# One inference step of a hybrid encoder on one core: two-tile stores, a weight sum in another block, and two pools for the down-projection

## The chip, the core and the metric

The kernel runs on one core of a Trainium2 chip. A core has a matrix engine (TensorE, PE in the profile, with its weight loads as PEld), a vector engine (VectorE, DVE), a scalar engine (ScalarE, ACT), a general one (GpSimd, POOL), and SyncE (SP), which issues most DMA transfers here. Each engine works through its own instructions in order and waits for the others by semaphores. The metric is the device time of one launch in microseconds (us); of several runs the median is given. The 0.2% below which two medians of this kernel can't be told apart is about 4.6 us.

## The reference

One layer over a prompt of 2048 tokens and 8 short sequences of 16 tokens, which together fill one more tile: 17 tiles of 128 tokens with 1024 features, all in float32.

```python
qm, km, vm, om, ip, fp, qa, ka, va = split_in(x @ w_in)
hm, C1, n1, m1 = mlstm_chunkwise(qm, km * 128**-0.5, vm, ip + b_i, log_sigmoid(fp + b_f), C0, n0, m0, chunk)
hm = sigmoid(om) * head_norm(hm, g_mlstm_norm)           # 4 heads x 128
ha = sliding_window_attention(rope(qa), rope(ka), va, sinks)   # 8 query heads, 2 key heads x 64
mix = concat(hm, ha) @ w_out
h = layer_norm(alpha * x + mix)
u = h @ w_up                                              # 1024 -> 5632 = value | gate
c = b_conv + sum(ext(u)[:, j:j + T] * w_conv[j] for j in range(3))
y = layer_norm(alpha * h + (silu(gate(c)) * value(c)) @ w_down)   # 2816 -> 1024
```

The outputs are y, the new mLSTM states, the new keys and values, and the last rows of u.

## The kernel before, in words

The work has four stages, which follow one another on TensorE.

1. *Input projection*, 0 to about 621 us. Four blocks of four token tiles (`IBLOCKS`; the tile of the short sequences, number 16, belongs to the first). Within a block, five groups g = 0 to 4: two for queries and keys of the mLSTM, one for the attention's queries (zqa), one for the output gates (zog), one for the mLSTM's values (zv). Each group is a 2x2 block product done with seven products instead of eight (Strassen's scheme in Winograd's form), in the order s = 1, 7, 6, 2, 5, 3, 4, into three PSUM banks (`i_product`, the matmuls of L713). `i_after` combines the products, and `i_store` (L757 and following) writes each finished quarter, 2 token tiles by 256 columns, to DRAM. `i_direct` (L739) computes the narrow columns: the gates' inputs and the attention's keys and values (`i_keys`, whose store is L750).
2. *Output projection*, about 622 to 899 us (L223 to L225), with the first layer norm.
3. *Up-projection* with the convolution, about 899 to 1827 us (L1883); its result, value times gate, goes to DRAM (`zf`, store L1971).
4. *Down-projection*, about 1827 to 2300 us (L2091; L2099 copies a product that two results share into a second PSUM bank, and L2122 adds into the results' accumulators `yacc`), again with seven products.

Each float32 operand is split into a high and a low part (L218 casts the high part on ScalarE, L219 subtracts it on VectorE), and three matmuls are done for each product.

Into the first stage the tiles' own work is woven as generators that a planner (`Chains`) advances between steps of two matmul groups, by costs and due times: for each tile an mLSTM chain (gates' logarithms L1007 to L1010, their transposes on TensorE at L1019, the head norm's statistics L1171 to L1178, transposes at L1188, the numerator L1223, the state L1235) and an attention chain (scores, L1332, L1354 and L1355, L1360); for the short sequences `t_sample` (softmax with sinks L1515 to L1527).

The order of TensorE's instructions is written out by hand (a manual schedule). The other engines' instructions are ordered when the program is built, by a list scheduler that takes the program's order, dependences and buffer lifetimes into account; each engine then runs its list in order. SP's list is the queue of nearly all loads and stores: where an issue waits for a buffer or for data, everything behind it waits as well.

Two further parts belong to the change. Down-projection products with the combined quarters of `wdn` need sums of its rows. Four slices of them are formed in the first stage by `d_sums(k, step)`, called after product s = 6 (step 0: two loads of 512 KB into buffers `txy`, L854 and L855), after s = 5 (step 1: four VectorE subtractions, L860 to L863) and after s = 3 (step 2: two stores to `zt`, L865 and L866). The buffers are those of `xr1` and `xr3`, two tiles that the loads of the next block's inputs use too. The pairs (b, g) at which this happens stand in one line of `i_dense`, with nb = 4 blocks:

```python
if (b, g) in ((nb - 2, 1), (nb - 1, 0), (nb - 1, 1), (nb - 1, 2)):
```

And the down-projection reads `zf` back in quarters r1 to r4 (`d_load`, issued at L2013). r1 lies in a buffer of the outer pool `fsb`; r2, r3, r4 and the accumulators `yacc` lie in the pool `dsb`, which is opened when the up-projection's pools `f2sb` and `f3sb` are closed and takes their place in SBUF. The weights of the down-projection come at L2031.

Of the kernel before, what the change touches and what calls it, by code (L numbers as in the profile page):

```python
# [8 lines left out]
F32 = mybir.dt.float32  # L9
# [5 lines left out]
P = 128  # L15
D = 1024
# [5 lines left out]
NT = NPT + 1  # L22
# [18 lines left out]
IBLOCKS = [[0, 1, 2, 3, 16], [4, 5, 6, 7], [8, 9, 10, 11], [12, 13, 14, 15]]  # L41
# [6 lines left out]
HT = 2 * P  # L48
# [157 lines left out]
class Prog:  # L206
# [20 lines left out]
    def run(self):  # L227
        PS = bass.MemoryType.PSUM
        nb = len(OBLOCKS)
        with ExitStack() as es:  # L230
            def enter(*a, **k):
                cm = self.pool(*a, **k)
                return cm.__enter__(), cm
            close = lambda cm: cm.__exit__(None, None, None)
            self.cp = es.enter_context(self.pool("const"))
            self.dp = es.enter_context(self.pool("dram", space=bass.MemoryType.DRAM))
            es.enter_context(self.tc.manual_schedule(engines={mybir.EngineType.PE}))
            self.setup()
            self.wp = es.enter_context(self.pool("wsb"))
            self.dps = es.enter_context(self.pool("dps", 3, PS))  # L240
            self.tp, tcm = enter("tsb", side="right")
            self.tps, tpcm = enter("tps", 5, PS)
            self.xp, xcm = enter("xsb")
            self.mp, mcm = enter("isb")
            chains = Chains(self)
            self.xs, self.gates, self.i_done = {}, {}, 0
            self.i_begin()
            self.warm_up()
            chains.weave(self.i_dense())
            close(mcm)  # L250
            wx, wxcm = enter("wx1sb")
            self.unit_more(wx)
            self.mp, mcm = enter("osb")
            self.o_setup()
            for b in range(nb - 1):
                chains.weave(self.late_done(self.o_block(b)))
            chains.until(NPT - 1)
            chains.drain()
            close(tpcm)
            close(tcm)  # L260
            self.fp, fcm = enter("fsb", side="right")
            self.fup, fpcm = enter("fup", 3, PS)
            self.f_setup()
            dense = self.o_block(nb - 1)
            first = self.f_hT(0)
            next(first)
            n = 0
            for i, _ in enumerate(dense):
                if i >= 2:
                    next(first, None)  # L270

                if i in (4, 7, 10):
                    self.f_tokens(0, *{4: (1,), 7: ("t1",), 10: ("t3", 7, "t2", 6)}[i])

                if i >= 22 and n < (2, 4, 5)[min((i - 22) // 4, 2)]:
                    self.f_next()
                    n += 1
            for _ in first:
                pass
            assert not self.norms  # L280
            close(mcm)
            close(wxcm)
            close(xcm)

            self.wx, wxcm = enter("wx2sb")
            self.f2, f2cm = enter("f2sb")
            self.f3, f3cm = enter("f3sb")
            self.f_ups(n)
            close(f3cm)
            close(f2cm)  # L290
            self.f2, f2cm = enter("dsb")
            self.f_downs()
            for cm in (f2cm, wxcm, fpcm, fcm):
                close(cm)


    def setup(self):
        nc, a, cp, dp = self.nc, self.a, self.cp, self.dp
        self.ident = cp.tile([P, P], F32, name="ident")
        self.eps = cp.tile([P, 1], F32, name="eps")  # L300
        nc.vector.memset(self.eps, EPS)
        self.mhalf = cp.tile([P, 8], F32, name="mhalf")
        nc.vector.memset(self.mhalf, -0.5)
        self.zqk = [dp.tile([8, P, P * len(b)], F32, name=f"zqk{i}") for i, b in enumerate(IBLOCKS)]
        self.zws = [[dp.tile([1 if g < KEPT else 2, P, 4, HT], F32, name=f"zws{g}_{i}") for i in range(4)] for g in range(NG)]
        self.zv = [dp.tile([P, 512], F32, name=f"zv{t}") for t in range(NT)]
        self.zog = [dp.tile([P, 512], F32, name=f"zog{t}") for t in range(NT)]
        self.zqa = [dp.tile([P, 512], F32, name=f"zqa{t}") for t in range(NT)]
        self.zkv = [dp.tile([P, 256], F32, name=f"zkv{t}") for t in range(NT)]
        self.zmix = [dp.tile([KD, P, P * len(b)], F32, name=f"zmix{i}") for i, b in enumerate(OBLOCKS)]  # L310
        self.zh = [dp.tile([P, D], F32, name=f"zh{t}") for t in range(NT)]
        self.zw = [dp.tile([4, P, 1024], F32, name=f"zw{j}") for j in range(NFF)]
        self.zc = [dp.tile([P, 2, len(FBLOCKS[0]) * P], F32, name=f"zc{j}") for j in range(NFF)]
        self.zM = [dp.tile([1, MH, P + 1], F32, name=f"zM{i}") for i in range(2)]
        self.zt = dp.tile([2, NK2, P, D], F32, name="zt")
        self.zf = [dp.tile([NFF, P, len(b) * P], F32, name=f"zf{i}") for i, b in enumerate(FBLOCKS)]
# [274 lines left out]
    def i_dense(self):  # L591
        nc, a = self.nc, self.a
        nb = len(IBLOCKS)
# [34 lines left out]
        for item in self.items:  # L628
# [9 lines left out]
            if item[0] == "t":  # L638
                _, b, ti, e = item
# [22 lines left out]
            _, b, g, s = item  # L662
# [25 lines left out]
            with self.tc.issue_after(behind) if behind and b == 0 else nullcontext():  # L688
                self.advance()

            if (b, g) in ((nb - 2, 1), (nb - 1, 0), (nb - 1, 1), (nb - 1, 2)):

                steps = (6, 5, 3)
                if s in steps:
                    self.d_sums(sums, steps.index(s))
                    sums += s == steps[2]
# [55 lines left out]
    def i_store(self, b, g, i, j, ev):  # L752

        nc = self.nc
        v = ev.rearrange("p (c m) -> p c m", c=2)
        if g < 2:
            f = 4 * i + 2 * g  # L757
            nc.sync.dma_start(self.zqk[b][f:f + 2, :, j * HT:(j + 1) * HT].rearrange("f p m -> p f m"), v)
        else:
            z = (self.zqa, self.zog, self.zv)[g - 2]  # L760
            for c in range(2):
                nc.sync.dma_start(z[IBLOCKS[b][2 * j + c]][:, i * HT:(i + 1) * HT], v[:, c])

    def i_out(self, b, g, i, j, src):

# [1236 lines left out]
    def d_load(self, b, q, u):  # L2002

        h, one = self.d_shape(b)
        if u == 0:
            pool, tag = (self.fp, "hraw") if q == 1 else (self.f2, f"r{q}")
            self.dr[b, q] = pool.tile([P, NK2, 384], F32, name=f"r{q}", tag=tag, bufs=1)
        r = self.dr[b, q]
        k0 = 0 if q in (1, 3) else NK2
        c0 = 0 if q in (1, 2) else h  # L2010
        ks = slice(DUNITS[u][0], DUNITS[u][-1] + 1)
        z = self.zf[b][k0:k0 + NK2][ks].rearrange("k p m -> p k m")
        self.nc.sync.dma_start(r[:, ks, :h], z[:, :, c0:c0 + h])  # L2013
        if one and q in (1, 2):
            self.nc.sync.dma_start(r[:, ks, h:h + one], z[:, :, 2 * h:])
# [46 lines left out]
            self.d_load(*l)  # L2062

    def f_downs(self):
        nc, a, f2 = self.nc, self.a, self.f2
        V, S = nc.vector, nc.scalar
        mm = nc.tensor.matmul
        ln2 = []
# [9 lines left out]
        nb, nu = len(FBLOCKS), len(DUNITS)  # L2078
        ys, ops = {}, {}
# [63 lines left out]
        for g, (b, s, u) in enumerate(self.dseq):  # L2143
# [3 lines left out]
            ts = [*tiles[:np_], *tiles[2 * np_:]] if s == 1 else tiles[np_:2 * np_] if s == 2 else []  # L2147
            if 0 <= u - 2 < len(ts):
                t = ts[u - 2]
                ys[t] = f2.tile([P, D], F32, name="yacc", tag="yacc", bufs=6)  # L2150
                nc.sync.dma_start(ys[t], self.zh[t])
            if g == 3 * nu:
                for n in ("ln2_g", "ln2_b"):
                    t = self.fp.tile([P, D], F32, name="f_" + n, tag="hst", bufs=2)
# [53 lines left out]
```

## Time and profile before

| | |
|---|---|
| median of 3 runs | 2300.78 us (2300.11 to 2303.31) |
| profiled execution, its own time | 2301.44 us |
| its span in the profile | 2299.7 us |
| mean granted TensorE clock | 0.998 |
| busy: PE / PEld / DVE / ACT / POOL | 99% / 91% / 79% / 55% / 12% |
| DMA: moved, mean rate | 631.30 MB, 275 GB/s |

Share of busy time says what an engine did, and not what it waited for. Where one engine is busy nearly all the time, the rows to read are its waits: each gives the engine and line that waited, the engine, tile and line that released it, the time in total, how often, and the longest. The timeline gives an instruction's start in us from the span's start, its length, engine, line, operation, the tiles written and read with their shapes, and in brackets the idle time ahead of it with its releaser; SPq is SP's queue of DMA issues. A window gives the busy time of each engine in a stretch, with the number of instructions, then the granted clock as a share of full speed, the DMA engines' share and the rate in GB/s. DMA rows give the tile written and read, the queue, the number of issues, the size and the median time to landing.

### The profile page before, as it was taken

How to read it: one execution, taken by the hardware profiler on the slowest of the kernel's cores; microseconds unless marked ns; L12 is line 12 of the kernel's file. 1: busy time of each engine (PE TensorE's matmuls, PEld its weight loads, DVE VectorE, ACT ScalarE, POOL GpSimd, SP SyncE). 2: the span in 40 equal slices, each digit the busy share in tenths (PEclk: the TensorE clock that was granted, in tenths of full speed). 3: DMA queues.
4: the chain of work that ended last, by engine and by line, in shares of the span. 5: the costliest groups of instructions: out<-in, count | busy, mean ns of one | idle time of the engine just before them, and what ended most of it. 6: DMA issues, size and time to landing. Idle time of an engine off the chain costs nothing.

```text
span 2299.7 us, 39828 instructions
## 1 busy us (share of the span) xinstructions
PE 2275.3 (99%) x14293; PEld 2090.5 (91%) x14293; DVE 1810.8 (79%) x3068; ACT 1272.3 (55%) x2373; POOL 277.5 (12%) x509
## 2 busy tenths in 40 slices
PE   8999999999999999999999999999999999999998
PEld 8999999989878778999999999999999978888876
DVE  8787677777688888998778777678766786895987
ACT  5453476766776656555656555556555544444442
POOL 0001001010121210211112000003211200200100
PEclk9999999999999999999999999999999999999999
DMA  7988998899998867898777999988998786757742
GB/s 283 318 304 289 302 327 276 276 309 305 324 324 266 279 212 279 300 331 300 280 273 269 305 300 310 311 267 288 320 295 262 248 298 212 251 173 222 256 153 86
DMA packets 302901, 631.30 MB, mean 275 GB/s; under 512 B 48172, under 2 KB 141424, under 8 KB 302704
## 3 DMA queue, kind: packets, MB, share of 16 engines
q1 hardware_dynamic: 298032, 615.06, 79.1%
q0 software_dynamic: 3520, 10.56, 1.5%
q10 hardware_dynamic: 1152, 3.15, 0.4%
q8 instruction: 113, 1.85, 0.3%
q14 instruction: 84, 0.69, 0.1%
HBM read 457.02 MB, written 171.64 MB: 273 GB/s over the span
## 4 chain that ended last, share of the span: by engine, by line
PE 84%; DVE 2%; DMA 2%; issue 0%; ACT 0%; POOL 0%; SPq 0%; DVEq 0%; POOLq 0%; ACTq 0%
PE dps L1883 20%; PE fup L1883 20%; PE dps L713 9%; PE dps L2091 7%; PE fup L2091 6%; PE fht L2091 6%; PE dps L223 3%; PE dps L225 2%; PE dps L224 2%; PE ppo L1360 1%; PE psc L1315 1%; PE ppt L1354 1%; PE dps L739 1%; PE fht L1707 1%; PE pscore L1140 1%; PE pnum L1223 1%
## 5 line engine op out<-in xcount | busy, mean ns | idle before, releaser
L1883 PE MATMUL fup<-hh,uw 128*128 128x384 f32 (+1 forms) x1848 | 478.2, 328 | 0.0
L1883 PE MATMUL dps<-hh,uw 128*128 128x384 f32 (+1 forms) x1848 | 478.0, 328 | 0.0
L1883 PEld LDWEIGHTS fup<-hh,uw 128*128 128x128 f32 x1848 | 330.3, 188 | 0.0
L1883 PEld LDWEIGHTS dps<-hh,uw 128*128 128x128 f32 x1848 | 330.1, 188 | 0.0
L1883 PE MATMUL fup<-hl,uw 128*128 128x384 f32 (+1 forms) x924 | 302.9, 328 | 0.9 <-DVE hl L219 0.9
L1883 PE MATMUL dps<-hl,uw 128*128 128x384 f32 (+1 forms) x924 | 302.8, 328 | 0.0
L1941 DVE SCALAR_TENSOR_TENSOR cc<-u,cw,cc 128x768 f32<-128x768 f32 (+1 forms) x264 | 258.1, 978 | 38.8 <-ACT cc L1939 30.5
L713 PE MATMUL dps<-w,oh 128*128 128x256 f32 x1344 | 254.7, 285 | 0.0
L218 ACT CAST uw<-wraw 128x1024 fp32r<-128x1024 f32 x126 | 123.2, 978 | 230.1 <-PE dps L2091 122.2
L219 DVE TENSOR_TENSOR w<-wraw,w 128x1024 fp32r<-128x1024 f32 (+2 forms) x163 | 186.3, 1150 | 65.7 <-ACT w L218 63.3
L218 ACT CAST w<-wraw 128x1024 fp32r<-128x1024 f32 (+2 forms) x163 | 160.2, 991 | 114.1 <-PE dps L713 53.6
L713 PEld LDWEIGHTS dps<-w,oh 128*128 128x128 f32 x1344 | 210.8, 188 | 11.0 <-issue 8.1
L219 DVE TENSOR_TENSOR uw<-wraw,uw 128x1024 fp32r<-128x1024 f32 x126 | 142.4, 1131 | 62.1 <-ACT uw L218 61.9
L713 PE MATMUL dps<-w,ol 128*128 128x256 f32 x672 | 188.2, 280 | 0.0
L1883 PEld LDWEIGHTS fup<-hl,uw 128*128 128x128 f32 x924 | 173.6, 188 | 1.7 <-DVE hl L219 1.6
L2091 PE MATMUL fup<-uw,fu 128*128 128x512 f32 x726 | 173.9, 396 | 1.3 <-ACT fht L2099 1.3
L1883 PEld LDWEIGHTS dps<-hl,uw 128*128 128x128 f32 x924 | 173.8, 188 | 0.0
L713 PE MATMUL dps<-oh,w 128*128 128x256 f32 x896 | 167.6, 283 | 2.9 <-DVE w L219 2.2
L2091 PEld LDWEIGHTS fup<-uw,fu 128*128 128x128 f32 x726 | 136.5, 188 | 34.3 <-ACT fht L2099 1.8
L2091 PE MATMUL dps<-uw,fu 128*128 128x512 f32 x660 | 164.9, 396 | 0.0
L2091 PEld LDWEIGHTS dps<-uw,fu 128*128 128x128 f32 x660 | 124.2, 188 | 29.7
L713 PEld LDWEIGHTS dps<-oh,w 128*128 128x128 f32 x896 | 140.0, 188 | 9.6 <-issue 4.9
(320 smaller groups left out, 4569.0 us busy)
## 6 DMA issues: line engine op xcount, KB each, us to landing
uw<-zw SPq DMA_DIRECT2D x176, 512.0 KB, 4.8
zw<-uw SPq DMA_DIRECT2D x88, 512.0 KB, 3.5
w<-zws SPq DMA_DIRECT2D x72, 512.0 KB, 6.0
wv<-wup SPq DMA_DIRECT2D x66, 512.0 KB, 5.0
wraw<-wi SPq DMA_DIRECT2D x65, 512.0 KB, 5.2
wraw<-zt SPq DMA_DIRECT2D x60, 512.0 KB, 3.8
wraw<-wdn SPq DMA_DIRECT2D x45, 512.0 KB, 4.5
wraw<-wo SPq DMA_DIRECT2D x40, 512.0 KB, 4.7
```

The costliest lines, as they stand in the source:

```text
L218: nc.scalar.copy(hi, src)
L219: return nc.vector.tensor_sub(lo, src, hi.bitcast(F32)).ins
L223: mm(out, ah, bh, start=start, stop=False)
L224: mm(out, ah, bl, start=False, stop=False)
L225: mm(out, al, bh, start=False, stop=stop)
L713: mm(o, l, r, start=s in (1, 7) and c == k == i == 0, stop=k == 3 and i == 2, skip_group_check=True)
L739: mm(o, x, w, start=k == i == 0, stop=k == KD - 1 and i == 2, skip_group_check=True)
L1140: self.nc.tensor.matmul(ps[:, h], qk[:, 4 + h], qk[:, h], start=True, stop=True)
L1223: nc.tensor.matmul(ps[:, i], sd[:, h], v1[:, h], start=True, stop=t == 0)
L1883: mm(ps, l[:, k], r[:, k], start=s in (1, 7) and k == 0 and i == 0, stop=k == 3 and i == 2, skip_group_check=True)
L1941: V.scalar_tensor_tensor(c[:, v], u[:, i:i + n], w[i], c[:, v], op0=ALU.mult, op1=ALU.add)
L2091: mm(ps, l[:, k, c], r[:, k], start=s in (1, 4, 7) and u == 0 and k == 0 and i == 0, stop=u == nu - 1 and k == n - 1 and i == 2, skip_grou ...
```

## The change

Three parts.

*Stores.* A quarter of groups 2 to 4 covers two neighbouring tiles of a block. Before, each tile has its own DRAM tensor for zqa, zog and zv, and a quarter is stored by two transfers of 128 KB. After, each block has one DRAM tensor with the tile number ahead, and one transfer of 256 KB stores both; readers get slices of it by tile.

*Sums.* The four sums of `wdn` rows stand at (2,1), (3,0), (3,1), (3,2) before and at (1,1), (2,1), (3,0), (3,2) after. The slices are taken in order, so the second sum's slice is now formed at (2,1), and so on.

*Pools.* Instead of one pool `dsb` laid over both pools of the up-projection, `d2sb` (r2 and r3) and `d3sb` (r4 and `yacc`) are opened one after the other in the place of `f2sb` and `f3sb`.

```diff
@@ run
             close(f3cm)
             close(f2cm)
-            self.f2, f2cm = enter("dsb")
+            self.f2, f2cm = enter("d2sb")
+            self.f3, f3cm = enter("d3sb")
             self.f_downs()
-            for cm in (f2cm, wxcm, fpcm, fcm):
+            for cm in (f3cm, f2cm, wxcm, fpcm, fcm):
                 close(cm)
@@ setup
-        self.zv = [dp.tile([P, 512], F32, name=f"zv{t}") for t in range(NT)]
-        self.zog = [dp.tile([P, 512], F32, name=f"zog{t}") for t in range(NT)]
-        self.zqa = [dp.tile([P, 512], F32, name=f"zqa{t}") for t in range(NT)]
+        self.zo = [[dp.tile([len(b), P, 512], F32, name=f"{n}{i}") for i, b in enumerate(IBLOCKS)] for n in ("zqa", "zog", "zv")]
+        self.zqa, self.zog, self.zv = [{t: z[i][ti] for i, b in enumerate(IBLOCKS) for ti, t in enumerate(b)} for z in self.zo]
@@ i_dense
-            if (b, g) in ((nb - 2, 1), (nb - 1, 0), (nb - 1, 1), (nb - 1, 2)):
+            if (b, g) in ((1, 1), (nb - 2, 1), (nb - 1, 0), (nb - 1, 2)):
@@ i_store
-            z = (self.zqa, self.zog, self.zv)[g - 2]
-            for c in range(2):
-                nc.sync.dma_start(z[IBLOCKS[b][2 * j + c]][:, i * HT:(i + 1) * HT], v[:, c])
+            z = self.zo[g - 2][b][2 * j:2 * j + 2, :, i * HT:(i + 1) * HT]
+            nc.sync.dma_start(z.rearrange("c p m -> p c m"), v)
@@ d_load
-            pool, tag = (self.fp, "hraw") if q == 1 else (self.f2, f"r{q}")
+            pool, tag = (self.fp, "hraw") if q == 1 else (self.f3 if q == 4 else self.f2, f"r{q}")
@@ f_downs
-        nc, a, f2 = self.nc, self.a, self.f2
+        nc, a = self.nc, self.a
...
-                ys[t] = f2.tile([P, D], F32, name="yacc", tag="yacc", bufs=6)
+                ys[t] = self.f3.tile([P, D], F32, name="yacc", tag="yacc", bufs=6)
```

## The prediction

> **What bounds the kernel.** I read the page first (busy times, clock), then the waits sorted by length, TensorE's first, then the stretches around each long wait in the timeline and the windows.
>
> ```profile
> PE 2275.3 (99%) x14293; PEld 2090.5 (91%) x14293; DVE 1810.8 (79%) x3068; ACT 1272.3 (55%) x2373; POOL 277.5 (12%) x509
> ...
> PE ppt L1354 <- ACT pth L1355: 2.7, 1, 2.7
> ...
> PE pht L1188 <- ACT hn L1178: 1.3, 3, 0.5
> PE fup L2091 <- ACT fht L2099: 1.3, 1, 1.3
> PE pnum L1223 <- issue: 1.0, 1, 1.0
> ...
> PE ppt L1527 <- POOL scs L1521: 0.8, 1, 0.8
> PE ppt L1354 <- DVE C L1235: 0.8, 1, 0.8
> ```
>
> TensorE (PE) is busy for 99% of the span, and the change leaves its instructions and their order as they are. So time can only come from TensorE's few waits, or go into new ones. The rows are: engine, what waited, who released it, total us, times, longest. The list also has waits for first weights, at the start and in the first block, which the change leaves alone; those shown add up to 7.9 us, and the rest of the text places each.
>
> **The change, part by part.** I compared the order in which the built programs issue on each engine. TensorE's is identical. VectorE (DVE) and ScalarE (ACT) differ only near five places, SyncE's queue (SP) throughout.
>
> *Stores of two tiles by one transfer.* 48 pairs of 128 KB stores become 48 stores of 256 KB. Nearest rows (KB, then median us to landing):
>
> ```profile
> zqk<-zev SPq DMA_DIRECT2D x32, 256.0 KB, 4.1
> ...
> zv<-zev SPq DMA_DIRECT2D x32, 128.0 KB, 4.4
> ```
>
> A transfer of the new size already lands as fast as one of the old. No TensorE wait above comes from these stores or from what reads them, so I take 0 for the 48 issues saved (below: at most a few tenths either way, through the order of SP's queue). They are what lets SP issue other loads earlier; that is counted where those loads are used.
>
> *One weight sum moved from the last block to the second.* A sum is two loads (L854, L855), four VectorE subtractions (L860 to L863) and two stores (L865, L866). Before, the four sums of this stage lie one in the third block, three in the last; after, one in the second, one in the third, two in the last. This touches four places.
>
> Place 1, the last sum of the last block, 498 to 521 us. Windows (PE, PEld, DVE, ACT, POOL busy, then granted PE clock, DMA share, GB/s) and timeline (start, us):
>
> ```profile
> 511.00:514.20 3.20, 0.54 (x6) 0.30 (x4) 1.82 (x3) 1.82 (x6) 1.35 (x1) 1.00 1.04 382
> 514.20:517.40 3.20, 3.20 (x9) 1.26 (x10) 2.05 (x3) 3.20 (x8) 0.38 (x2) 0.51 0.86 297
> ...
> 487.75 0.69 DVE L860 TENSOR_TENSOR txy<-txy 128x512 f32<-128x512 f32 x1 [1.74 <-DMA txy<-wdn]
> ...
> 498.34 0.33 SPq L854 DMA_DIRECT2D txy<-wdn  x1
> ...
> 505.89 0.33 SPq L855 DMA_DIRECT2D txy<-wdn  x1
> ...
> 499.45 0.68 DVE L784 SCALAR_TENSOR_TENSOR zev<-dps,zev 128x512 f32<-128x512 f32 x1
> 503.93 0.69 DVE L860 TENSOR_TENSOR txy<-txy 128x512 f32<-128x512 f32 x1 [3.79 <-DMA txy<-wdn]
> ...
> 512.38 1.28 ACT L1178 ACTIVATE hn<-hn,ms 128x128 f32<-128x128 f32 x4 [2.32 <-POOL ms L1172]
> 513.56 1.04 ACT L1355 COPY pth<-ppt 128x512 f32<-128x512 f32 x2
> 514.18 1.06 PE L1354 MATMUL ppt<-ident,sc 128*128 128x128 f32 x4 [2.66 <-ACT pth L1355]
> ```
>
> VectorE works in order. It stands 3.79 us before L860 for a load that went out only when the previous sum's store had left the buffer, and the norm statistics of the token tile are queued behind. They reach ScalarE late (L1178), which makes L1355 late, for which TensorE waits 2.7 us, after 0.8 us for L1235. Then, in the second window, TensorE works at a granted clock of 0.51: 3.2 us of which 0.49 is lost, 1.6 us. So this place costs 0.8 + 2.7 + 1.6 = 5.1 us. With only two sums in the last block, the later one takes the position that the earlier of the two removed from here had (the row at 487.75: a VectorE wait of 1.74, which delayed no TensorE instruction), and between 499 and 513 VectorE has none of this work. L1178 could then start 3.8 + 0.7 = 4.5 us earlier, at 507.9, and L1355 at 509.1; TensorE wants its result from 514.18 − 2.66 = 511.5 on, so the wait goes altogether. Ends: 0 and −5.1. I take −5.0.
>
> Place 2, the sum of the third block, 306 to 334 us:
>
> ```profile
> 312.37 0.69 DVE L860 TENSOR_TENSOR txy<-txy 128x512 f32<-128x512 f32 x1 [2.76 <-DMA txy<-wdn]
> ...
> 330.51 0.16 DVE L1171 TENSOR_TENSOR mr<-mr,bmv 128x4 f32<-128x4 f32 x1
> ...
> 318.73 1.13 PE L1223 MATMUL pnum<-v,dt 128*128 128x129 f32 x8 [1.00 <-issue]
> ...
> 333.94 0.62 PE L1188 MATMUL pht<-ident,hn 128*128 128x128 f32 x2 [0.48 <-ACT hn L1178]
> ```
>
> Here too VectorE waits for the load, 2.76 us, and TensorE then misses 1.0 us (L1223) and 1.3 us (three waits for L1178): 2.3 us. After, both loads go out some 7 us earlier on SP, and all four subtractions stand earlier in VectorE's order, in front of the running sums of the gates. The wait goes, but a reciprocal that needs ScalarE's exponentials moves ahead of the statistics and costs VectorE about 1 us. So L1171 comes 2.76 − 1.0 = 1.7 us earlier. Ends 0 and −2.3; I take −1.7.
>
> Place 3, the new sum in the second block, 165 to 178 us. In the built order L860 stands right behind L880 at 169.19, the other three between there and L1010, and one more L219 moves ahead of L1010. L1010 ends the gate logarithms that TensorE transposes at L1019, with nothing to overtake it.
>
> ```profile
> DMA to landing us min/median/max: 2.7/5.9/8.2
> ...
> 165.18 0.32 SPq L750 DMA_DIRECT2D zkv<-zev  x1
> ...
> 169.19 0.28 DVE L880 TENSOR_TENSOR zev<-zev,ropet 128x128 f32<-128x128 f32 x1
> ...
> 173.49 1.22 DVE L219 TENSOR_TENSOR w<-wraw,w 128x1024 fp32r<-128x1024 f32 x1
> 174.63 0.38 DVE L1007 SCALAR_TENSOR_TENSOR gl<-gl,gl 128x16 f32<-128x16 f32 x2
> ...
> 175.25 0.17 DVE L1010 SCALAR_TENSOR_TENSOR g<-gl,g 128x16 f32<-128x16 f32 x1
> ...
> 177.95 0.27 PE L1019 MATMUL pgr<-ident,g 128*4 128x128 f32 x1
> ```
>
> The first row is that of this sum's transfers (tile txy). The first load follows the store of 165.18, so goes out at 165.6 and lands 5.9 later, at 171.5; VectorE is there at 169.5: 2.0 us of waiting. Four subtractions at 0.65 (0.69 less overlap) are 2.6, the L219 is 1.14 (to the start of the next): 5.7 us. Against it stand 175.42 to 177.95, 2.5 us of slack, and 0.2 of idle time before an L219. TensorE waits 3.0 us. By the shortest landing (2.7) there is no VectorE wait and it is 1.0; by the longest (8.2) it is 5.3. Below 1.0 is excluded as the instructions stand in front of L1010. I take 3.0, the median's. What queues behind: the weight splits L219, which have three products (8 us) of lead, the sample tile's state update, and on SP the two zt stores, which hold the next weight loads for one or two us. I cost these at nothing; without that cover, see the second rival.
>
> [...]
>
> Place 4, the sample tile's softmax. L551 and the rotary add L881 now stand ahead of L1515.
>
> ```profile
> 246.92 0.15 DVE L1515 SCALAR_TENSOR_TENSOR amx<-amx,nsinkx 128x4 f32<-128x4 f32 x1
> 247.00 1.22 DVE L551 TENSOR_TENSOR wraw<-xr 128x1024 f32<-128x1024 f32 x1
> 248.13 0.68 DVE L881 TENSOR_TENSOR zev<-zev,rb 128x512 f32<-128x512 f32 x1
> ...
> 247.85 0.30 ACT L1516 ACTIVATE aes<-amx,k_sinkx 128x4 f32<-128x4 f32 x1
> ```
>
> L1515 comes 1.1 + 0.6 = 1.7 us later less 0.2 of idle time, at 248.4, but ScalarE began its successor only at 247.85: the chain to L1521, for which TensorE already waits 0.8, is 0.6 us longer. Ends 0 and +1.7; I take +0.6.
>
> *Two pools in the down-projection.* Before, its first new loads sit in a pool laid over both pools of the up-projection, so they wait until the last of those is read, a store:
>
> ```profile
> 1836.60 0.43 SPq L1971 DMA_DIRECT2D zf<-cc  x1
> 1842.33 4.33 SPq L2013 DMA_DIRECT2D r<-zf  x8
> ...
> 1845.78 0.83 ACT L218 CAST fu<-r 128x768 fp32r<-128x768 f32 x1 [4.59 <-DMA r<-zf]
> ...
> 1851.28 1.06 ACT L2099 COPY fht<-fup 128x512 f32<-128x512 f32 x2
> ...
> 1851.91 18.41 PE L2091 MATMUL fup<-uw,fu 128*128 128x512 f32 x78 [1.31 <-ACT fht L2099]
> ...
> 1852.00:1855.20 3.20, 3.20 (x14) 2.62 (x15) 2.20 (x3) 2.98 (x5) 0.00 (x0) 1.00 1.06 409
> ```
>
> ScalarE idles 4.59 us for those loads and then does the casts in one go, so L2099 comes late and TensorE waits 1.31. After, r2 and r3 lie over the first of the old pools alone: in the built order five r loads stand ahead of the last zf store and wait for engines only, some 10 us earlier. ScalarE can cast as the buffers come free, and L2099 is in time. r4 and yacc still wait for the store, and the remaining weights (L2031) now stand behind them on SP; by the 18.41 us of the matmul group that starts at 1851.91 the first of them is needed after 1870, so they are next in line but not late. (The last row is the window behind this wait, with the clock at 1.00.) Ends 0 and −1.3 (the wait shown); I take −1.3.
>
> **Sum.** −5.0 − 1.7 − 1.3 + 0.6 + 3.0 = −4.4 us. The profiled execution took 2301.44 us by its own time (span 2299.7), 0.66 above the median of the runs, 2300.78. So 2297.0 against the profile and 2296.4 against the median. A measurement of this kernel tells 0.2%, 4.6 us, from no change: faster means below 2296.2.
>
> **Rivals.**
> - The new wait at L1019 also halves the clock. For: the wait of 2.7 us at place 1 was followed by 3.2 us at 0.51. Against: after the wait of 1.31 it stood at 1.00 (the window at 1852), and the forecast wait is little longer than 2.7. Price 1.6 us: 2298.0. [...]
> - Slower: the sum is only moved, and SP carries the loss. If the loads land late at place 3 (8.2 us), VectorE loses 4.3 us there, the zt stores hold SP, and weight loads behind them come late as well. Place 1 shows such a blocked queue: 498.34 to 505.89 between two loads of one sum, 5.1 us lost on TensorE. Price: 5.3 at L1019, 1.6 of clock, 5.1 for weights, 1.7 (the upper end) at place 4, against gains of 8.0: +5.7, 2306.5. It decides once the new waits together exceed 8.0. Against: the sum at 487.75 had a VectorE wait of the same kind, and TensorE shows no wait for it in the list.
> - The load lands early, or VectorE catches up: the wait at L1019 stays at 1.0, giving 2294.4. For: SP reaches the load with 48 fewer stores on its way; against: the DMA share of 0.9 to 1.0 in the windows shown.
> - The change doesn't do what it says: the waits are only passed on (place 1's sum waits where it now stands, or r loads come no earlier). Without −5.0 it is 2301.4, without −1.3 it is 2297.7.
>
> **How the numbers follow.** Forecast, 2296.4: 0.40, half of it on either side of 2296.2. Clock halved: 0.18, nearly all of it within 0.2%. Early load: 0.16, faster. Waits passed on: 0.12, within 0.2%. Slower rival: 0.14. Faster 0.20 + 0.16 + 0.04 from the second case with a smaller wait = 0.40; slower (over 2305.4) 0.12, as the slower rival with a little less falls short of that bound; within 0.2% the rest, 0.48. The range from 2292.0 (early load, with place 2 worth 2.3, place 4 nothing, and a little less at L1019) to 2303.0 (place 1's gain missing and the clock halved) leaves out most of the slower rival and some 0.05 at the other end; the forecast's own is 2294 to 2298.5.
>
> **What would show it.** Right: no wait of L1354 for L1355 near 514 us and no window at 0.51 there; L1223 without a wait near 318; L2091 without one for L2099; r loads before the last zf store; a new TensorE wait at L1019 near 178, released by VectorE's L1010, of about 3 us. Wrong: L1019 without wait, or a clock below 1 behind it; waits of L713 for VectorE's w between 178 and 200 us (the slower rival); a stall kept at 500 to 520 us.

## The result, and the profile after

The changed kernel takes 2294.61 us (median of 7 runs, 2293.15 to 2295.48) against 2302.19 us before (7 runs, 2300.11 to 2303.31). The ratio is 0.9969, 95% interval 0.9960 to 0.9978: faster by 0.31%. The prediction was 2296.4 with a range of 2292.0 to 2303.0. Its time was close, in part by luck: the forecast change was −4.4 us and the measured one is −7.6, but the median of before that the forecast started from, 2300.78, is now 1.4 us higher. Of its steps, one was wrong outright (place 3) and two were put down to the wrong part of the change (places 2 and 4).

The profiled execution of the changed kernel has a span of 2292.1 us, 7.6 less than that of before. Lines of the changed kernel behind L760 carry a number one lower than before (L1010 is now L1009). First TensorE's waits by length, in the changed kernel (engine, line waited for, total us, times, longest):

```profile
PE ppt L1526 <- POOL v L1104: 1.4, 1, 1.4
PE dps L713 <- ACT mr L1164: 1.0, 1, 1.0
...
PE pnum L1222 <- issue: 0.3, 1, 0.3
PE pht L1187 <- ACT hn L1177: 0.3, 1, 0.3
```

The 2.7 us of L1354 for L1355 (now L1353 and L1354) are gone from the list, and so is L2091's wait for L2099. The sample softmax, 0.8 before, is 1.4 now (the row names a small GpSimd memset that ended just behind the product L1520). A wait of 1.0 is new.

Both traces hold the same 14293 matmuls in the same order. So the start of the same matmul can be subtracted between two profiles, and how the difference moves over a stretch is what that stretch gained or lost. I worked these shifts out from the rows of TensorE in each trace. By them, against the first profile of before:

| stretch of before, us | step of the prediction | forecast | measured |
|---|---|---|---|
| 0 to 160 | none | 0 | −0.2 |
| 160 to 245 | place 3, the new sum | +3.0 | 0.0 |
| 245 to 260 | place 4, sample softmax | +0.6 | +0.5 |
| 300 to 340 | place 2, sum of the third block | −1.7 | −0.7 |
| 498 to 524 | place 1, last sum | −5.0 | −5.7 |
| 1835 to 1860 | join, two pools | −1.3 | −1.5 |
| all else together | none | 0 | +0.1 |
| sum (of unrounded terms) | | −4.4 | −7.6 |

The windows of these stretches, the kernel before (busy time of PE, PEld, DVE, ACT, POOL with instructions, granted clock, DMA share, GB/s):

```profile
305.00:335.00 30.00, 27.67 (x240) 26.27 (x239) 19.82 (x61) 18.80 (x50) 2.52 (x6) 1.00 0.98 335
498.00:521.00 23.00, 19.50 (x143) 16.10 (x142) 14.26 (x33) 14.04 (x34) 2.98 (x4) 0.93 0.85 288
1835.00:1855.00 20.00, 18.68 (x80) 14.80 (x80) 10.97 (x12) 10.84 (x14) 0.00 (x0) 1.00 0.95 306
```

and of the changed kernel:

```profile
305.00:335.00 30.00, 28.37 (x245) 27.07 (x245) 20.74 (x62) 19.64 (x52) 2.52 (x6) 1.00 1.00 342
498.00:521.00 23.00, 23.00 (x191) 20.67 (x189) 15.21 (x47) 17.20 (x45) 2.03 (x5) 1.00 0.97 321
1835.00:1855.00 20.00, 20.00 (x88) 16.14 (x87) 13.56 (x15) 9.66 (x14) 0.00 (x0) 1.00 1.01 360
```

Around 510 us TensorE now works without a gap at full clock, 191 matmuls where there were 143. At the join it is busy throughout. Five of the r loads now stand ahead of the last zf store on SP (changed kernel), so that ScalarE begins its casts of them at 1830.89 us, where the first one stood at 1845.78 before:

```profile
1824.94 3.02 SPq L2012 DMA_DIRECT2D r<-zf  x5
...
1833.88 0.43 SPq L1970 DMA_DIRECT2D zf<-cc  x1
```

Between 305 and 335 us little has changed.

### The profile page after: what moved, and what is told of

It is laid out like the page before. It is cut to its first block, busy times and chain, and to the rows that moved or that the text cites. A ratio compares the mean times of both kernels' runs of the same rounds, so it can differ in the third digit from the quotient of the medians.

```text
span 2292.1 us, 39775 instructions
## 1 busy us (share of the span) xinstructions
PE 2273.5 (99%) x14293; PEld 2090.7 (91%) x14293; DVE 1809.8 (79%) x3068; ACT 1272.4 (56%) x2373; POOL 278.7 (12%) x509
## 4 chain that ended last, share of the span: by engine, by line
PE 83%; DVE 3%; issue 1%; ACT 1%; DMA 1%; POOL 0%; SPq 0%; DVEq 0%; ACTq 0%; POOLq 0%
PE dps L1882 20%; PE fup L1882 20%; PE dps L713 8%; PE fup L2090 7%; PE dps L2090 7%; PE fht L2090 6%; PE dps L223 3%; PE dps L225 2%; PE dps L224 2%; PE ppo L1359 1%; PE ppt L1353 1%; PE psc L1314 1%; PE fht L1706 1%; PE pcu L1231 1%; PE dps L739 1%
```

## The experiments

Every experiment is shown as its edit, what was expected, and what came out. Ratios are to the kernel before on the same chip. Shifts are against the first profile of before unless another is named.

### Each part alone

The sum alone:

```diff
-            if (b, g) in ((nb - 2, 1), (nb - 1, 0), (nb - 1, 1), (nb - 1, 2)):
+            if (b, g) in ((1, 1), (nb - 2, 1), (nb - 1, 0), (nb - 1, 2)):
```

> The kernel before, with the one line of the sums changed to (1,1), (2,1), (3,0), (3,2); stores and pools as before. Theory 1, the moved sum carries the gain of the first stage by itself: TensorE gains 5.7 us between 498 and 521 us, as in the whole change, and the join at 1850 keeps its wait of 1.3; 5.0 to 6.6 us less than before, ratio 0.9971 to 0.9978. Theory 2, the merged stores carry it, as they shorten SP's queue ahead of the sum's loads: TensorE still waits over 2 us for L1355 near 514, and the gain is under 2 us (ratio over 0.999). In both, no wait at L1019 near 178 us, since the transposes there read the gates of the first block.

Measured: 2297.85 us, ratio 0.9981 (0.9971 to 0.9990). The stretch 498 to 524 gains 5.6 us, all of the changed kernel's gain there. The stretches at places 2 and 4 move by 0.0, and so does that of place 3. 470 to 498 us loses 0.6 here (a wait ahead of L1223, which the changed kernel doesn't have). TensorE's waits, of this run:

```profile
PE pnum L1223 <- issue: 1.5, 2, 1.0
PE pht L1188 <- ACT hn L1178: 1.3, 3, 0.5
...
PE ppt L1527 <- POOL scs L1521: 0.8, 1, 0.8
...
PE fup L2091 <- ACT fht L2099: 0.7, 1, 0.7
```

The waits of place 2 (L1223 and L1188) and the 0.8 of place 4 are as before. So theory 1 holds at place 1, though the ratio lies just above its 0.9971 to 0.9978 and the wait at the join was 0.7 and not 1.3. Whatever happens at places 2 and 4 in the changed kernel is not the moved sum's.

The two pools alone:

```diff
-            self.f2, f2cm = enter("dsb")
+            self.f2, f2cm = enter("d2sb")
+            self.f3, f3cm = enter("d3sb")
```

(with the lines of `d_load` and `f_downs` that go with it)

> The kernel before, with the two pools alone. Theory 1: the change up to 1800 us is nothing, and at the join TensorE's wait of 1.3 us for L2099 goes, 1.5 us less than before, ratio 0.9993. Theory 2, the gain at the join needs the earlier parts (SP's queue must be ahead): the wait stays over 0.5 us, and the time is that of before to 0.5 us.

Measured: 2301.36 us, ratio 0.9994 (0.9984 to 1.0003). The join gains 1.54 us and its wait is gone from the list. By the time alone this can't be told from no change; by the trace theory 1 holds. The span is 2.6 us shorter than in the first profile: 0.9 of it fell at 505 us, where this edit changes nothing. That is taken up with the repeated profile below.

The stores alone: the changed kernel with the old list of sums and the old pool.

```diff
-            z = (self.zqa, self.zog, self.zv)[g - 2]
-            for c in range(2):
-                nc.sync.dma_start(z[IBLOCKS[b][2 * j + c]][:, i * HT:(i + 1) * HT], v[:, c])
+            z = self.zo[g - 2][b][2 * j:2 * j + 2, :, i * HT:(i + 1) * HT]
+            nc.sync.dma_start(z.rearrange("c p m -> p c m"), v)
```

(with the lines of `setup` that go with it)

> The kernel before, with the merged stores alone. Theory 1, the saved issues are worth nothing by themselves: no term over 1 us at any place, the waits at 514 and 1850 stay at 2.7 and 1.3, total within 1 us of before (ratio 0.9995 to 1.0005); the 0.5 us lost at 252 us may show here, if the stores move L551. Theory 2, the stores carry part of the first stage's gain: 2 us or more off at 498 to 521 us, ratio under 0.9992.

Measured: 2299.75 us, ratio 0.9990 (0.9980 to 0.9999). Its waits of TensorE (line numbers are one or two lower than before here):

```profile
PE ppt L1352 <- ACT pth L1353: 2.7, 1, 2.7
...
PE ppt L1525 <- POOL v L1103: 1.4, 1, 1.4
PE fup L2089 <- ACT fht L2097: 1.1, 1, 1.1
...
PE dps L712 <- ACT mr L1163: 0.9, 1, 0.9
```

Here are the 1.4 of place 4 and the wait for `mr` that is new in the changed kernel. The shifts are +0.5 at place 4 and −1.6 at place 2. The first subtraction of the third block's sum, here and then with the sum alone:

```profile
306.60 0.68 DVE L858 TENSOR_TENSOR txy<-txy 128x512 f32<-128x512 f32 x1
```

```profile
311.96 0.69 DVE L860 TENSOR_TENSOR txy<-txy 128x512 f32<-128x512 f32 x1 [2.52 <-DMA txy<-wdn]
```

With the stores merged, the sum's two loads go out at 299.3 and 302.0 us, and VectorE no longer waits for them; with the sum alone they go out at 305.9 and 308.1, about as before. 470 to 498 loses 0.9; the changed kernel, with the same stores, doesn't, so no run shows whose term that is. 498 to 524 gains 1.0, but 0.3 of it is a shorter wait for L1235 and some 0.7 the clock, which is not halved in this execution (next experiment). Neither theory is quite right: the stores have terms of their own of either sign, over 1 us at place 2, though they aren't what cures place 1. The three ratios' gains (0.19, 0.06 and 0.10%) add up to 0.35%, near the 0.31% of the whole.

### The kernel before, profiled again

No edit.

> The kernel before, once more, with a profile of its own: which of the terms shown for it belong to the program and which to one execution. If the terms belong to the program, the same matmuls stand within 0.3 us of the first profile everywhere, TensorE waits 2.7 us for L1355 near 514 us, 0.8 for L1235 near 505 and 1.3 for L2099 near 1851, and the clock is at half behind the first of these. If they hang on when DMA transfers land in one execution, the waits near 505 and 1851 are 0.3 to 0.9 us shorter or gone, as in the runs with one part of the change, and the clock may stay at 1.00.

Measured: 2303.11 us, span 2301.3. Waits and windows of this execution:

```profile
PE ppt L1354 <- ACT pth L1355: 2.7, 1, 2.7
...
PE ppt L1354 <- DVE C L1235: 1.2, 1, 1.2
...
PE fup L2091 <- ACT fht L2099: 1.0, 1, 1.0
```

```profile
511.00:514.20 3.20, 2.00 (x18) 1.76 (x17) 3.13 (x6) 0.71 (x2) 2.50 (x1) 1.00 1.08 367
514.20:517.40 3.20, 1.70 (x9) 0.72 (x9) 0.96 (x3) 3.20 (x9) 0.38 (x2) 1.00 0.98 313
```

The wait for L1355 is the program's and comes again at 2.7. The clock behind it is not: it stays at 1.00. Still the stretch 498 to 524 differs by only 0.25 us between the two executions. At full clock the matmuls behind the wait take 1.5 us less. But this execution waits 0.4 longer for L1235, and the second group of L1360, which found its data ready where the clock was at half, waits 0.3 here and takes 0.5 longer (this execution's row at 520.57, then the first profile's at 520.30, both from the timeline):

```profile
520.57 1.56 PE L1360 MATMUL ppo<-pth,kva 128*64 128x512 f32 x4 [0.27 <-ACT pth L1355]
```

```profile
520.30 1.08 PE L1360 MATMUL ppo<-pth,kva 128*64 128x512 f32 x4
```

So half clock costs this stretch about 0.7 us net, and not 1.6. The wait for L1235 follows how long VectorE stands for the last sum's first load: 4.5 us and 1.2 of TensorE's here, 3.8 and 0.8 in the first profile, 3.6 and 0.5 with the stores alone, 3.4 and none with the pools alone. The wait for L2099 was 1.3 in the first profile, 1.0 here, and 0.7, 1.1 and 0.8 in three runs whose programs are alike at the join (the sum alone, the stores alone, and the next experiment). Between the two executions the first 12 us differ by 1.2 us, 620 to 900 by 0.7 and 1600 to 1700 by 0.6. So a term of about 1 us in one profile isn't yet the program's.

### The sums at their old places, in other buffers

```diff
-            pool = lambda q: (self.wp, "wraw", WR) if ring else (self.xp, f"xr{q}", 1)
+            pool = lambda q: (self.wp, "wraw", WR) if ring else (self.xp, f"xr{q + k % 2}", 1)
```

> The kernel before with all four sums at their old places, but every second sum in other buffers (the tags of the second and fourth quarter instead of the first and third), so that its loads needn't wait for the stores of the sum ahead. Theory 1, the loss near 514 us came from a load held up by the buffer: VectorE's wait of 3.8 us goes, and with it TensorE's 2.7 and the window at half clock, 4 to 6 us less than before (ratio 0.9974 to 0.9983). Theory 2, three sums are too much work for the last block, whatever their buffers: VectorE waits elsewhere, TensorE still loses 2 us or more between 480 and 530 us, under 3 us less than before (ratio over 0.9987).

Measured: 2298.32 us, ratio 0.9985 (0.9976 to 0.9994), between the two theories. The stretch 498 to 524 gains 3.4 us of the 5.7. Two rows of the timeline:

```profile
501.13 0.69 DVE L861 TENSOR_TENSOR txy<-txy 128x512 f32<-128x512 f32 x1 [2.47 <-DMA txy<-wdn]
...
511.38 0.66 PE L1354 MATMUL ppt<-ident,sc 128*128 128x128 f32 x4 [1.26 <-ACT pth L1355]
```

With the buffer free, the loads go out at 489.9 and 493.1 us instead of 498.3 and 505.9. The last sum's first subtraction comes 7.7 us earlier. But its second one now stands for 2.47 us ahead of the same statistics, and 1.3 of TensorE's 2.7 us stay. So the buffer was a part of the cause. The rest is that a sum's subtractions stand ahead of the statistics with a load that isn't there yet; only taking the sum out of this stretch takes all of it.

### The two pools in the other order

```diff
-            self.f2, f2cm = enter("d2sb")
-            self.f3, f3cm = enter("d3sb")
+            self.f3, f3cm = enter("d3sb")
+            self.f2, f2cm = enter("d2sb")
```

(closed in the order that goes with it)

> The changed kernel with its two pools of the down-projection in the other order, so that r4 and the accumulators lie lowest, and r2 and r3 over the second of the old pools. Theory 1, what counts is that r2 and r3 don't lie over the buffers that the last store reads: the r loads stand behind that store again, ScalarE idles over 3 us for them, TensorE waits 0.7 to 1.3 us for the copy of the shared product near 1850, and the span is 0.7 to 1.6 us longer than that of the changed kernel. Theory 2, it is enough that there are two pools: no wait there, span as the changed kernel's to 0.3 us.

Measured: 2296.41 us in one run, span 2294.6. Timeline and wait:

```profile
1836.99 10.48 SPq L2012 DMA_DIRECT2D r<-zf  x15
...
1839.98 1.05 ACT L218 CAST uw<-wraw 128x1024 fp32r<-128x1024 f32 x1 [3.15 <-DMA r<-zf]
1841.62 1.74 ACT L218 CAST fu<-r 128x768 fp32r<-128x768 f32 x2 [0.59 <-DMA r<-zf]
```

```profile
PE fup L2090 <- ACT fht L2098: 0.6, 1, 0.6
```

The r loads stand in one go behind the last store, ScalarE idles 3.7 us for them, the wait is back at 0.6 (a little under the expected 0.7 to 1.3), and the join is 0.9 us longer than in the changed kernel. Theory 1 holds in one execution: what helps is which buffers r2 and r3 lie over, and not that there are two pools. (Of the 2.5 us between the spans, 1.7 fell between 1600 and 1700 us, in the up-projection, which is alike in both.)

### Sums in other groups

The second sum at (1,2), later repeated beside the changed kernel, and at (2,2):

```diff
-            if (b, g) in ((1, 1), (nb - 2, 1), (nb - 1, 0), (nb - 1, 2)):
+            if (b, g) in ((1, 1), (1, 2), (nb - 1, 0), (nb - 1, 2)):
```

(in the other run `(nb - 2, 2)` stands for `(nb - 2, 1)`)

> The changed kernel with the sum of the third block, (2,1), at (1,2) instead: two in the second block, none in the third, two in the last. If the waits left between 305 and 340 us (0.3, 1.0 and 0.3 us) come from that sum's work ahead of the tile's statistics, they go, 1.2 to 1.8 us less than the changed kernel there; if they come from the tiles' chains themselves, they stay. Near 200 us, VectorE has 2.6 us more to do: by the theory that the weight splits' lead covers a sum, TensorE loses under 0.3 us there; by the rival, that two sums in succession wait for the first one's stores and hold the weights, 1 to 5 us.

> The changed kernel with the sum at (2,1) one group later, at (2,2). If the sum's work is the cause of the waits between 305 and 340 us, they go and 0 to 1.6 us come back in the group where it then stands (its VectorE work meets other statistics); if they are the chains' own, they stay. Between 2291 and 2296 us by either, so the profile decides.

> The changed kernel once more, beside the next one on the same chip. Its waits at 252 (1.4 us) and 326 us (1.0) belong to the program and come again; the terms of the start and of the up-projection may differ by up to 1.8 us in one execution. Ratio to the kernel before 0.996 to 0.998.

> The kernel with sums at (1,1), (1,2), (3,0), (3,2) once more. If the 2.0 us that its profile gains on the changed kernel between 305 and 340 us belong to the program, they come again there, and the median is 1 to 3 us below that of the changed kernel on this chip; if they are one execution's, the two medians agree to 1 us.

Measured: with (1,2), 2292.79 us, ratio 0.9965 (0.9953 to 0.9978); with (2,2), 2293.98, ratio 0.9968 (0.9957 to 0.9979). On one chip the changed kernel again took 2293.98 (ratio 0.9969, 0.9956 to 0.9981) and (1,2) again 2294.01 (0.9965, 0.9953 to 0.9978). None of them can be told from the changed kernel by its time. The windows say more. First the changed kernel, then (1,2):

```profile
305.00:325.00 20.00, 19.67 (x174) 18.80 (x174) 15.26 (x48) 12.38 (x37) 1.20 (x3) 1.00 0.99 340
```

```profile
305.00:325.00 20.00, 20.00 (x181) 19.50 (x180) 15.06 (x50) 14.36 (x41) 1.20 (x3) 1.00 1.01 359
```

Without a sum there TensorE has no gap, and 300 to 340 us is 2.0 us shorter than in the changed kernel. Between the two repeats the difference is only 0.5: the changed kernel's repeat gains 1.6 at place 2 instead of 0.7, and that of (1,2) still waits 0.4 for `mr` there (0.9 in the changed kernel). So the sum's work is a cause of what is left at place 2, of 0.5 to 2.0 us; the 2.0 us are in large part one execution's. And the second sum isn't free at its new place: 200 to 245 us loses 0.6, and in the repeat 160 to 245 loses 1.7 (a wait of 0.8 for an eviction on VectorE near 194). Place 4 is back at 0.8 with it. Moved to (2,2) in the program, a group later, the sum was placed by the scheduler only 2 to 6 us later (its subtractions at 308.0 to 316.3, against 305.6 to 310.4 in the changed kernel), and the waits stayed.

All four sums in the second block:

```diff
-            if (b, g) in ((1, 1), (nb - 2, 1), (nb - 1, 0), (nb - 1, 2)):
+            if (b, g) in ((1, 0), (1, 1), (1, 2), (1, 3)):
```

> The changed kernel with all four sums in the second block, at (1,0), (1,1), (1,2), (1,3). The slower rival of the prediction, made stronger: each sum's loads wait on SP for the stores of the one ahead, and the next block's inputs use the same buffers. If that rival's mechanism is real at this density, TensorE waits for weights (L713 for VectorE's w, or for DMA) or for L1019 between 165 and 290 us, 2 to 8 us in all, and the kernel is slower than the one with two sums there. If the lead of the weight splits covers it, nothing over 0.6 us shows, and the time is within 1 us of that one: sums that are early enough are free, whatever their number.

Measured: 2307.86 us, ratio 1.0028 (1.0018 to 1.0037), slower than the kernel before. Against the changed kernel TensorE loses 13.4 us between 200 and 340 us, more than the 2 to 8 expected. The longest of its new waits, and SP's queue there:

```profile
PE dps L713 <- DMA w<-zws: 4.7, 6, 2.0
...
PE dps L713 <- ACT gates L748: 1.9, 1, 1.9
PE dps L713 <- ACT zev L771: 1.8, 1, 1.8
```

```profile
269.37 0.46 SPq L541 DMA_DIRECT2D xr<-xq  x1
...
277.35 0.42 SPq L864 DMA_DIRECT2D zt<-txy  x1
277.83 0.42 SPq L865 DMA_DIRECT2D zt<-txy  x1
...
284.31 1.55 SPq L541 DMA_DIRECT2D xr<-xq  x2
```

The last sum, loaded at 251.5 and 252.3, holds `xr1` and `xr3` until its stores at 277; two of the next block's input loads go out only at 284, and the splits and weights behind them come late: TensorE waits 4.2 us in all between 293 and 316. Waits of 1.8 at 234 and of 3.4 in all for weights from 265 to 283 come earlier; SP carries loads and stores of the sums there too, but no run separates them. The last of these, 2.0 us, was followed by half clock (0.50 from 283.79 to 287.20). Inputs and weights held up on SP are the mechanism of the prediction's slower rival, at four sums where the change has one.

## Why the prediction was right and wrong

*Place 3, wrong: +3.0 forecast, 0.0 measured.* The step that failed is the sentence that L1010 "ends the gate logarithms that TensorE transposes at L1019". VectorE did come late, by 4.5 of the forecast 5.7 us (the wait for the first load was 1.1 us instead of 2.0; it was issued at 165.35, and VectorE could begin on it at 170.35). But TensorE didn't care. Timeline of the changed kernel:

```profile
170.35 0.69 DVE L859 TENSOR_TENSOR txy<-txy 128x512 f32<-128x512 f32 x1 [1.08 <-DMA txy<-wdn]
...
179.74 0.17 DVE L1009 SCALAR_TENSOR_TENSOR g<-gl,g 128x16 f32<-128x16 f32 x1
...
177.74 0.27 PE L1018 MATMUL pgr<-ident,g 128*4 128x128 f32 x1
```

The transposes ran at 177.74, two us before the logarithms that I had them wait for were written at 179.74. The tile `g` has two buffers, and these are different ones. The row for L1010 in the kernel before, as a group over the whole run, could have told it:

```profile
L1010 DVE SCALAR_TENSOR_TENSOR g<-gl,g x4: 171/174/176, 56.3 to 531.8; 128x16 f32<-128x16 f32 x3, 128x20 f32<-128x20 f32 x1
```

There are four of them, one for each block; the one of 128x20 has the five tiles of the first block and is formed at 56.3 us, over a hundred us before. The sample tile, whose gates L1019 transposes at 178, belongs to the first block. The logarithms formed at 175 are the second block's, of four tiles (128x16). The form was in the row that I quoted. This one term is nearly the whole difference: −4.4 − 3.0 = −7.4, and −7.6 was measured. That the rest comes out so small is luck, as the other errors cancel (place 1 −0.7, place 2 +1.0, the join −0.2, the start −0.2).

*Place 1, right: −5.0 and −5.7.* Against the three other executions with the sums at their old places and in their old buffers, the gain is 5.5, 4.8 and 4.7 (the repeat, the pools alone, the stores alone). The sum run shows that the moved sum alone does it, and the run with other buffers that the load's lateness is the lever, though not only through the buffer. One term of the sum was too large: half clock came in two of these four executions, and costs the stretch about 0.7 us net instead of 1.6. The 0.8 for L1235 was also no fixed term (0 to 1.2).

*Place 2, the mechanism right, the part of the change behind it wrong: −1.7 and −0.7.* It was put under the moved sum; the runs put it under the stores, as the sum alone leaves it at 0.0 and the stores alone give −1.6. The loads do go out about 7 us earlier. In the profile of the changed kernel VectorE still waits for the second one:

```profile
307.49 0.69 DVE L860 TENSOR_TENSOR txy<-txy 128x512 f32<-128x512 f32 x1 [0.76 <-DMA txy<-wdn]
```

In its repeat and with the stores alone there is no such wait, and both give −1.6; the run with the swapped pools gives −1.4. So the forecast size was nearly met in three of four executions. What I hadn't seen is the wait that follows: in the changed kernel ScalarE does the four scalings L1331 ahead of an eviction (L779), which ends 1.7 us later than before, and the next product waits 1.0 us. That wait appears in all four.

*Place 4, right: +0.6 and +0.5,* but again by the stores and not by the sum. So "merged stores: 0" was wrong as a heading: their terms by themselves were −1.6 and +0.5 at these places. What the 48 issues saved are worth by themselves, no run tells apart from the new order that the scheduler makes of the rest.

*The join, right: −1.3 and −1.5,* by the mechanism named: the swapped pools bring the wait back. Against the other executions without the pools the gain is 0.9 to 1.4, as the wait was 0.7 to 1.1 there.

*The rivals.* Faster, which came, had 0.40. The early load gave 2294.4, nearest to the measured 2294.6, but that is no support for it: the load came 1.1 us late for VectorE, and L1019 had no wait at all. Half clock behind a new wait: there was no new wait at L1019, though with four sums in a block a new one of 2.0 us was followed by it. Passed-on waits: none at place 1. The slower rival was priced with a delay at L1019 that can't occur, as what L1019 reads was written over 100 us before; but its other part, inputs and weights held up on SP, came true with four sums in a block.

## What to carry to other kernels

Before a wait is charged to an instruction, check that the reader and the writer have the same buffer: names and lines are alike for every block, forms and times are not. Where an order is made by a list scheduler, each part of an edit can move work anywhere that it shares a queue with, so run the parts alone, and compare the start of the same matmul in both traces rather than the medians; terms of 0.5 us are seen there that the times don't show. Take more than one execution of each, as terms of up to 1.7 us belonged to a single one here. And a sum that is moved out of a crowded stretch pays as long as its buffers are free again before the next user's loads: one was free here, two cost 0.6 to 1.7 us where they stood, four cost 13.4 us.

## What the runs showed of the hardware that was not expected

The same wait of 2.7 us was followed by half clock in two executions (the first profile of before, and the pools alone), and by 1.00 in two others (the repeat, and the stores alone). The traces show the difference. In each trace the granted clock changes only in steps of 3.41 us, whose place differs between executions: in the first profile it rises at 5.71, falls at 514.29 and rises at 517.70 us, and from 5.71 to 514.29 it is 149 times 3.413; in the changed kernel it rises at 7.77 and falls at 2287.87, 668 times 3.413 later. In the midst of a run the clock was at half six times in all these traces, each time for one such step. Here are two successive steps of the first profile, around the wait, and then two of the repeat, counted on from its changes at 5.97 and 9.38 us:

```profile
510.88:514.29 3.41, 0.75 (x7) 0.51 (x7) 1.94 (x3) 1.91 (x6) 1.47 (x1) 1.00 1.03 379
514.29:517.70 3.41, 3.41 (x11) 1.47 (x12) 2.11 (x3) 3.41 (x8) 0.38 (x2) 0.50 0.79 272
```

```profile
511.14:514.56 3.42, 1.86 (x17) 1.62 (x15) 3.20 (x5) 1.07 (x4) 2.50 (x1) 1.00 1.09 374
514.56:517.97 3.41, 2.27 (x13) 1.29 (x14) 1.10 (x3) 3.41 (x10) 0.38 (x2) 1.00 0.97 318
```

In the first profile the whole wait lies within one step, TensorE is idle for 2.7 of its 3.4 us, and the next step is at half. In the repeat a step ends in the midst of the wait, which is split into 1.6 and 1.1 us, and the clock stays. It is alike in the two other executions: 2.6 us in one step with the pools alone, 1.7 and 1.0 with the stores alone. Four sums in a block had 2.2 us of idle time in the step ahead of half clock. So what the wait of 2.7 us did to the clock went with the place of the steps, and the program doesn't set that: in the two executions of the kernel before, the changes begin at 5.71 and at 5.97 us. The step ahead of half clock need not be idle throughout: 2.2 us of 3.4 were enough, and in the first 12 us 1.1 to 1.6, though the 1.6 and 1.7 near 514 us were not. These runs show no one amount that decides.

Executions also differ at places where their programs are alike or nearly so: by up to 1.4 us in the first 12 us, 1.6 between 620 and 900 us, and 1.7 between 1600 and 1700. The first of these goes with the clock: three executions have half clock from about 9 us on (from 8.52, 9.38 and 10.11) and lose 0.8 to 1.2 us there against the first profile, the others lose nothing. In the up-projection TensorE waits in some executions for a copy on ScalarE (L1912, L1911 in the changed kernel: 0.3 us in the repeat, 0.5 and 0.4 with the pools swapped, 0.6 with (1,2)); what delays that copy stays open, as does the difference in the output projection.
